# Raw weight slots and split halves: nine and six instead of eleven and four, in a two-layer encoder with a mixture of experts

## The chip, the core and the metric

The kernel runs on one core of a Trainium2 chip. The metric is the device time of one execution in microseconds (us); lower is better. Engines are named as in the profile: PE multiplies matrices, DVE, ACT and POOL work elementwise, SP here only issues the transfers (DMAs) that bring weights from HBM into SBUF.

## The reference

A token sequence `x` (256 tokens, width 1024) and 256 memory tokens go through two layers: a convolution and pooling mixer, cross-attention and a dense SwiGLU in layer 0; a Conformer convolution module, cross-attention and a SwiGLU over eight experts with the top two per token in layer 1. Everything is float32. Cut to what matters here:

```python
def swiglu(xn, w_gu, w_down):
    g, u = jnp.split(xn @ w_gu, 2, axis=-1)
    return (jax.nn.silu(g) * u) @ w_down

def moe_swiglu(xn, router, w_gu, w_down):
    logits = (xn @ router).astype(jnp.float32)
    top_v, top_i = lax.top_k(logits, TOP_K)
    w = jax.nn.softmax(top_v, axis=-1)
    comb = jnp.sum(jax.nn.one_hot(top_i, N_EXPERTS) * w[..., None], axis=-2)
    for e in range(N_EXPERTS):
        out = out + comb[..., e:e + 1] * swiglu(xn, w_gu[e], w_down[e])
    return out

h = h + even_mixer(...)              # layer 0
h = h + cross_attn(...); h = h + swiglu(...)
h = h + conformer_conv(...)          # layer 1
h = h + cross_attn(...); h = h + moe_swiglu(...)
return rmsnorm(h, final_norm)
```

## The kernel before

**Chunks.** All large weights come in chunks of 128 partitions by 2048 float32 (1 MB) through `load` (L143), which takes a slot of the pool `rawp` (tag "raw", `NRAW` = 11 slots, L86) or, for some chunks of the experts, a "spare" tile of the pool `big`, and issues the DMA on SP.

**Splitting.** PE multiplies in a rounded format, so that each weight w is used as a high part hi (w rounded) and a remainder lo (w minus hi). `split` (L152) makes both for the two halves of a chunk: ACT casts hi (L168), DVE subtracts for lo (L169). A half of hi is a tile of `hip`, a half of lo one of `lop`, both with `NPART` = 4 slots (L87, L88), so two chunks stand split at a time. A raw slot is free again when the DVE has made the last lo from it; a pair of halves is free when PE has used it.

**Other users of raw slots.** In the last product of layer 0 (`ffn_down`, L685 to L706) three chunks of `wv` are loaded and split beside it into `raw_pair` tiles (L198, class `Early`, L179): six raw slots, held until the values of layer 1 are multiplied (L803 to L828). The split of the last chunk of `wk` (L734) puts its second half into one more raw slot (`apart`, L161). The eight `pw1` chunks of the Conformer module are multiplied whole (`product_whole`, L250), out of their raw slots, which come free only when PE is done with them.

**The experts.** `expert` (L1112) runs eight times, with 42 chunks each: seven steps j, each with four chunks for gate and up (`gate_up`, L1117) and, one step behind, two for down (`down`, L1165). Such a group of six chunks is called a round below. Five experts are wide (positions 0, 1, 3, 5, 7 in this order): three matmuls per weight tile, 12 of 512 columns a chunk (`moving`, L207). Three are narrow (2, 4, 6): two matmuls, 8 a chunk (`narrow`, L1103), and the fourth chunk of a step is not split but multiplied whole (L1124). After the gate, ACT and DVE make the activation: L1141, L1142, L1143, L1144 and L1148 in a narrow expert, L1146 and L1148 in a wide one. L1148 needs the finished up product.

**What sets the order.** Most engines' queues are put in order when the program is made, by the framework's scheduler, which runs a plan of the kernel on its own clock and gives out slots in it; each engine then runs its queue in that order on the chip. From L857 on SP's order is written out by hand: the program's order of the loads. `RING` (L55) says which expert chunk takes a raw slot (r) and which a spare (s); from then on each chunk repeats the kind of the one `NRAW` + 6 = 17 before (L927), and so waits for that one's slot. `NAHEAD` (L58) is how many of these loads stand ahead of the attention's output product (L929).

Of the kernel before, what the change touches and what calls it, by code (L numbers as in the profile page):

```python
# [49 lines left out]
HALF = CAP // 2  # L50
TCKW = dict(schedule_with_timeline_sim=True)
NCKW = dict(dynamic_dma_scratch_size=512)
NRAW = 11
NPART = 4
RING = "rrrrrrrrsssssrrrrrs"  # L55
P2_POOL = (0, 2, 4, 6)
NWARM = 10
NAHEAD = 13  # L58
G_TAPS = 4 * (11, 12)


# [20 lines left out]
def _build(ctx, tc, io, cap):  # L82
    nc = tc.nc
    PSUM = bass.MemoryType.PSUM
    const = ctx.enter_context(tc.tile_pool(name="const", bufs=1))
    rawp = ctx.enter_context(tc.tile_pool(name="rawp", bufs=NRAW))  # L86
    hip = ctx.enter_context(tc.tile_pool(name="hip", bufs=NPART))  # L87
    lop = ctx.enter_context(tc.tile_pool(name="lop", bufs=NPART))  # L88
    big = ctx.enter_context(tc.tile_pool(name="big", bufs=10))
# [53 lines left out]
    def load(ap, n=CH, pieces=1, spare=False):  # L143
        raw = big_tile("spare") if spare else rawp.tile([P, CH], F32, tag="raw", name="raw")
        for i in range(pieces):
            sl = slice(i * n // pieces, (i + 1) * n // pieces)
            nc.sync.dma_start(raw[:, sl], ap[:, sl])
        return raw
# [772 lines left out]
    ahead = deque()  # L921
    kinds = list(RING)

    def fetch():
        n, (ap, pieces) = next(source)
        ahead.append(load(ap, pieces=pieces, spare=kinds[n] == "s"))
        kinds.append(kinds[-(NRAW + 6)])  # L927

    for _ in range(NAHEAD):  # L929
        fetch()  # L930
# [559 lines left out]
```

## Time and profile before

| what | value |
|---|---|
| time, median of 3 runs | 1550.54 us (1549.85 to 1551.14) |
| the profiled execution | 1551.01 us |
| its span | 1549.3 us |
| mean granted clock of PE | 0.994 of full speed |
| instructions | 23644 |
| read from HBM | 448.75 MB |

The page of the profile gives busy times and shares. The trace behind it is read by views: the sums of an engine's work in given stretches, the waits of one engine, the DMA issues, the timeline (instructions in order of time, with like ones merged as "x3", and in brackets the idle time before one and what ended it), and the chain of waits (the work that ended last, followed back from the end). Layer 0 takes about the first 390 us, the Conformer module and the attention run to about 594 us, the experts from there to about 1535 us. PEld is PE's loading of stationary tiles, SPq the SP queue.

### The profile page before, as it was taken

To read this page: it belongs to the slowest core of one execution; us is meant where nothing else is said; L and a number is where in the kernel's file an instruction comes from. 1 tells how busy PE (TensorE), PEld (TensorE's weight loads), DVE (VectorE), ACT (ScalarE), POOL (GpSimd) and SP (SyncE) were. 2 spreads that over 40 slices of the span, in tenths; PEclk is the share of its full clock that TensorE was granted. 3 is DMA by queue.
4 is the path that set the end of the run, shared out by engine and by line. 5 is a ranking of instruction groups with operands and counts; after the bars stand their busy time and mean duration, and the time that the engine had idled before them with its cause. 6 is when DMAs were issued, how large, how long until landed. Compare 5 with 4: busy or idle time off the path is not lost.

```text
span 1549.3 us, 23644 instructions
## 1 busy us (share of the span) xinstructions
PE 1513.3 (98%) x8558; PEld 1295.2 (84%) x8558; DVE 1298.1 (84%) x1730; ACT 1052.1 (68%) x1381; POOL 149.0 (10%) x230
## 2 busy tenths in 40 slices
PE   8899999999999999999999999999999999999996
PEld 8899999999998998888888778888667888667885
DVE  7866677776898868989989989889889888889897
ACT  6454554455575657777777877777777777777775
POOL 4710000001294210000000000000000000000000
PEclk9999999999999999999999999999999999999998
DMA  9654454436545566999999999999999999999940
GB/s 371 266 181 159 146 176 166 138 98 226 210 137 222 186 254 217 378 370 335 373 374 336 402 422 407 382 364 341 406 395 378 370 362 341 403 398 371 387 177 30
DMA packets 65214, 451.43 MB, mean 291 GB/s; under 512 B 7360, under 2 KB 7488, under 8 KB 12480
## 3 DMA queue, kind: packets, MB, share of 16 engines
q1 hardware_dynamic: 65088, 449.83, 76.7%
q8 instruction: 69, 1.13, 0.3%
q14 instruction: 57, 0.47, 0.1%
HBM read 448.75 MB, written 1.05 MB: 290 GB/s over the span
## 4 chain that ended last, share of the span: by engine, by line
PE 81%; DVE 9%; POOL 3%; issue 3%; ACT 2%; DMA 1%; SPq 0%; DVEq 0%; POOLq 0%; ACTq 0%
PE gu L211 8%; PE gu L212 8%; PE gu L216 8%; PE acc L205 7%; PE acc L204 7%; PE acc L203 7%; DVE lo L169 7%; PE gu L1124 5%; PE gu L1108 4%; PE py L211 4%; PE py L216 4%; PE py L212 4%; PE py L1108 3%; POOL part L764 2%; PE gx L1027 1%
## 5 line engine op out<-in xcount | busy, mean ns | idle before, releaser
L169 DVE TENSOR_TENSOR lo<-raw,hi 128x1024 fp32r<-128x1024 f32 (+3 forms) x573 | 671.0, 1208 | 120.1 <-ACT hi L168 110.4
L168 ACT CAST hi<-raw 128x1024 fp32r<-128x1024 f32 (+3 forms) x573 | 565.6, 1031 | 213.5 <-PE acc L204 92.0
L169 DVE TENSOR_TENSOR lo<-spare,hi 128x1024 fp32r<-128x1024 f32 (+1 forms) x226 | 261.4, 1203 | 24.6 <-ACT hi L168 20.5
L168 ACT CAST hi<-spare 128x1024 fp32r<-128x1024 f32 (+1 forms) x226 | 221.5, 1036 | 23.6 <-PE gu L212 11.9
L211 PE MATMUL gu<-hi,xg 128*128 128x512 f32 x560 | 218.8, 391 | 0.0
L212 PE MATMUL gu<-hi,xg 128*128 128x512 f32 x560 | 218.4, 390 | 0.0
L216 PE MATMUL gu<-lo,xg 128*128 128x512 f32 x560 | 154.2, 391 | 0.7 <-DVE lo L169 0.7
L216 PEld LDWEIGHTS gu<-lo,xg 128*128 128x128 f32 x560 | 104.7, 188 | 23.9 <-DVE lo L169 1.9
L211 PEld LDWEIGHTS gu<-hi,xg 128*128 128x128 f32 x560 | 105.1, 188 | 22.2 <-ACT hi L168 0.2
L212 PEld LDWEIGHTS gu<-hi,xg 128*128 128x128 f32 x560 | 105.1, 188 | 21.8
L211 PE MATMUL py<-hi,ht 128*128 128x512 f32 x280 | 111.1, 398 | 0.0
L212 PE MATMUL py<-hi,ht 128*128 128x512 f32 x280 | 109.3, 390 | 0.0
L205 PE MATMUL acc<-a2h,lo 128*128 128x256 f32 x336 | 95.2, 283 | 0.0
L204 PE MATMUL acc<-a2l,hi 128*128 128x256 f32 x336 | 95.2, 283 | 0.0
L203 PE MATMUL acc<-a2h,hi 128*128 128x256 f32 x336 | 95.1, 283 | 0.0
L1386 POOL TENSOR_TENSOR fo<-accum,fn 128x512 f32<-128x512 f32 x2 | 2.5, 1268 | 949.1 <-DVE accum L1190 949.1
L1108 PE MATMUL gu<-lo,xg 128*128 128x512 f32 x252 | 80.3, 411 | 8.0 <-DVE lo L169 8.0
L216 PE MATMUL py<-lo,ht 128*128 128x512 f32 x280 | 84.0, 395 | 0.0
L1108 PE MATMUL gu<-hi,xg 128*128 128x512 f32 x252 | 71.2, 396 | 0.0
L1108 PEld LDWEIGHTS gu<-lo,xg 128*128 128x128 f32 x252 | 43.4, 188 | 31.6 <-DVE lo L169 25.2
L203 PEld LDWEIGHTS acc<-a2h,hi 128*128 128x128 f32 x336 | 64.5, 192 | 0.0
L205 PEld LDWEIGHTS acc<-a2h,lo 128*128 128x128 f32 x336 | 64.5, 192 | 0.0
(421 smaller groups left out, 3176.9 us busy)
## 6 DMA issues: line engine op xcount, KB each, us to landing
raw<-in_moe_gu SPq DMA_DIRECT2D x139, 1024.0 KB, 7.1
spare<-in_moe_gu SPq DMA_DIRECT2D x85, 1024.0 KB, 7.2
raw<-in_moe_down SPq DMA_DIRECT2D x78, 1024.0 KB, 7.3
spare<-in_moe_down SPq DMA_DIRECT2D x32, 1024.0 KB, 7.0
raw<-in_ffn_gu SPq DMA_DIRECT2D x22, 1024.0 KB, 4.8
raw<-in_pw SPq DMA_DIRECT2D x12, 1024.0 KB, 4.9
raw<-in_ffn_down SPq DMA_DIRECT2D x16, 704.0 KB, 4.1
raw<-in_wk SPq DMA_DIRECT2D x8, 1024.0 KB, 7.1
```

Source lines behind the costliest of these rows:

```text
L168: done[:] = (S.copy(hi[:, i:i + step], raw[:, a + i:a + i + step]), V.tensor_sub(lo[:, i:i + step], raw[:, a + i:a + i + step], f32(hi[:, ...
L169: V.tensor_sub(lo[:, i:i + step], raw[:, a + i:a + i + step], f32(hi[:, i:i + step])))
L203: PE.matmul(ps, a[0], b[0], start=first, stop=False)
L204: PE.matmul(ps, a[0], b[1], start=False, stop=False)
L205: PE.matmul(ps, a[1], b[0], start=False, stop=last)
L211: PE.matmul(ps, a[0], b[0], start=first and i == 0, stop=False)
L212: PE.matmul(ps, a[1], b[0], start=False, stop=False)
L216: ins = PE.matmul(ps, a[0], b[1], start=False, stop=last and i == n - 1)
L764: G.tensor_add(part, part, prod)
L1027: PE.matmul(px[:, kk * P:(kk + 1) * P], xt[:, t * D + d0:t * D + d0 + P], oh[:, t, :], start=t == 0, stop=t == 1)
L1108: ins = PE.matmul(ps, x, w[part], start=first and i == part == 0, stop=last and part == 1 and i == n - 1)
L1124: PE.matmul(pz, f32(xs[kk]), w[:, kk * 512:(kk + 1) * 512], start=False, stop=kk == 3)
```

## The change

Two raw slots of 8 KB per partition are given up, and two halves each of hi and lo, of 4 KB per partition each, are added. Three chunks can then stand split instead of two. The pattern of kinds is shortened to a period of 15 (9 raw slots and 6 spares), and one load less stands ahead of the output product.

```diff
-NRAW = 11
-NPART = 4
-RING = "rrrrrrrrsssssrrrrrs"
+NRAW = 9
+NPART = 6
+RING = "rrrrrrrsssssrrrrs"
...
-NAHEAD = 13
+NAHEAD = 12
```

## Rows read from the trace of the kernel before

**Rows 1.** The page's part 1: busy us, share of the span, instructions.

```profile
PE 1513.3 (98%) x8558; PEld 1295.2 (84%) x8558; DVE 1298.1 (84%) x1730; ACT 1052.1 (68%) x1381; POOL 149.0 (10%) x230
```

**Rows 2.** Stretches: us, busy PE, PEld, DVE, ACT, POOL, clock, DMA, GB/s.

```profile
100.00:400.00 300.00, 300.00 (x2417) 296.03 (x2416) 206.76 (x322) 156.55 (x241) 14.67 (x16) 1.00 0.48 163
...
717.00:832.00 115.00, 115.00 (x526) 95.20 (x525) 105.44 (x101) 89.69 (x96) 0.00 (x0) 1.00 0.96 359
...
1065.00:1175.00 110.00, 105.85 (x438) 72.76 (x437) 94.32 (x98) 83.07 (x101) 0.00 (x0) 1.00 0.97 383
1185.00:1297.00 112.00, 111.80 (x525) 92.81 (x524) 100.95 (x97) 83.97 (x93) 0.00 (x0) 1.00 0.97 365
```

**Rows 3.** SP's own waits: us in total, times, longest.

```profile
SPq L147 <- DVE lo L169: 839.0, 307, 14.6
```

**Rows 4.** DMA issues: count, KB each, median us to landing.

```profile
raw<-in_moe_gu SPq DMA_DIRECT2D x139, 1024.0 KB, 7.1
...
raw<-in_pw SPq DMA_DIRECT2D x12, 1024.0 KB, 4.9
```

**Rows 5.** Timeline of SP in expert 2: two loads.

```profile
847.42 0.33 SPq L147 DMA_DIRECT2D spare<-in_moe_gu  x1
...
876.43 0.33 SPq L147 DMA_DIRECT2D spare<-in_moe_gu  x1
```

**Rows 6.** Timeline in expert 2: PE and ACT take these chunks.

```profile
886.25 3.59 PE L1124 MATMUL gu<-spare,xg 128*128 128x512 f32 x8
...
907.90 2.01 ACT L168 CAST hi<-spare 128x1024 fp32r<-128x1024 f32 x2
```

**Rows 7.** Chain of waits in expert 2: whole chunks, steps 3-6.

```profile
886.41 3.43 PE gu L1124 x8
...
899.41 3.43 PE gu L1124 x8
...
913.08 3.45 PE gu L1124 x8
...
928.64 3.43 PE gu L1124 x8
```

**Rows 8.** Chain of waits in expert 4: whole chunks, steps 1, 6.

```profile
1085.45 3.45 PE gu L1124 x8
...
1163.60 3.43 PE gu L1124 x8
```

**Rows 9.** Timeline of DVE in expert 4, step 3.

```profile
1118.11 1.22 DVE L169 TENSOR_TENSOR lo<-spare,hi 128x1024 fp32r<-128x1024 f32 x1 [1.72 <-ACT hi L168]
1120.06 0.75 DVE L1148 SCALAR_TENSOR_TENSOR eh<-gu,cw,esg 128x512 f32<-128x512 f32 x1 [0.73 <-PE gu L1124]
```

**Rows 10.** Timeline of ACT in expert 4, around L1141 of step 4.

```profile
1122.55 5.79 ACT L168 CAST hi<-raw 128x1024 fp32r<-128x1024 f32 x6
...
1129.91 0.59 ACT L1141 COPY esg<-gu 64x512 f32<-64x512 f32 x1 [1.57 <-PE gu L1108]
...
1132.62 1.98 ACT L168 CAST hi<-raw 128x1024 fp32r<-128x1024 f32 x2
```

**Rows 11.** Timeline of ACT in expert 2, around L1141 of step 4.

```profile
895.80 2.00 ACT L168 CAST hi<-spare 128x1024 fp32r<-128x1024 f32 x2 [0.88 <-PE gu L1108]
898.09 0.58 ACT L1141 COPY esg<-gu 64x512 f32<-64x512 f32 x1 [0.29 <-PE gu L1108]
```

**Rows 12.** Timeline of ACT in the wide experts 1 and 3.

```profile
756.78 2.96 ACT L168 CAST hi<-raw 128x1024 fp32r<-128x1024 f32 x3 [0.58 <-PE gu L212]
...
1013.52 0.69 ACT L1146 ACTIVATE esg<-gu,cw 128x512 f32<-128x512 f32 x1 [2.37 <-PE gu L216]
```

**Rows 13.** Timeline of PE and of SP in the Conformer module.

```profile
399.23 34.70 PE L255 MATMUL acc<-a,raw 128*128 128x256 f32 x160
...
434.20 7.07 PE L255 MATMUL acc<-a,raw 128*128 128x256 f32 x32
...
405.75 50.56 SPq L147 DMA_DIRECT2D raw<-in_pw  x10
```

## The prediction

> **What bounds the kernel now.** I read the page first: PE is busy in nearly the whole span, but DVE is not far behind [rows 1], so the shares alone do not say who waits for whom. The sums by stretch separate the regimes [rows 2]. In layer 0 (100 to 400 us) PE is busy for all of its 300 us and the transfers use half of the DMA engines' time. In the wide expert 1 PE is again busy for the whole stretch; in the narrow expert 4 it is not (105.85 of 110 us), and neither DVE (94.32) nor ACT (83.07) is full. The DMA share of 0.96 or 0.97 there tempts one to call the experts bound by transfers. Three views say no. SP's waits are for DVE's lo, that is, for a slot to come free: 839 us in 307 waits [rows 3]. So it is the slots that hold the loads back. A load lands 7.1 us after its issue in the median [rows 4]; the one issued at 847.42 us [rows 5] is multiplied whole at 886.25 [rows 6], 39 us later, and the one issued at 876.43 [rows 5] is cast at 907.90 [rows 6], 31.5 us later. The second is about the tightest chunk in the experts, and it still lies ready for some 24 us.
>
> What does bound a narrow expert is read from its rounds. On the chain of waits the whole chunks of expert 2 follow each other by 13.0 and 13.7 us, and then by 15.56 [rows 7]; in expert 4 five rounds from 1085.45 to 1163.60 take 78.15, or 15.63 each [rows 8]. Expert 6 is like expert 4. A late round thus costs 15.6 - 13.3 = 2.3 us more than an early one (13.3 is the mean of the first two). The timeline shows where: DVE stands still for 1.72 us until ACT has cast the next hi, and for 0.73 us behind L1148, which needs the up product [rows 9]; together 2.45. ACT is late because L1141, which waits 1.57 us for PE, stands ahead of those casts in its queue [rows 10]. In the early rounds of expert 2 the casts stand ahead of L1141 [rows 11].
>
> **The change part by part.** The sum is made on the profiled execution, 1551.01 us (span 1549.3 and 1.7 around it); the median of the runs is 0.47 lower.
>
> *Two raw slots fewer, in the experts.* A chunk could be loaded 17 + 2 = 19 ahead of PE (slots and split chunks), and afterwards 15 + 3 = 18. One chunk less is 2.2 to 2.6 us less of lead (a round of 13.3 or 15.6 over six chunks); two chunks less, where the third split chunk is not in use, are at most 5.2. The tightest chunk keeps over 18 us. What hides this is the ready ring, and the cost is 0. Were that cover gone, a chunk would cost what is left of its 7.1 us landing [rows 4].
>
> *A third split chunk, in wide experts and layer 0.* ACT does wait for PE to free halves there (0.58 us in expert 1 [rows 12]), so ACT and DVE will run further ahead. But PE, the one that ends the stretch, has no gap to give back: 115.00 of 115 us, and 300.00 of 300 [rows 2]. In the wide expert 3 ACT runs with less lead (it waits 2.37 us for PE at L1146 [rows 12]), and expert 5, in the same order, still has PE busy in 111.80 of 112 us [rows 2]. So lead is worth at most the 0.2 us left, in each wide expert. Cost 0, bounds -1 and 0.
>
> *A third split chunk, in late narrow rounds.* This decides the sign. The casts behind L1141 do not wait for a pair of halves: once ACT gets to them at 1132.62 no wait stands before them [rows 10], and their chunks landed long ago. They stand late because the queue was written so. The six casts at 1122.55 [rows 10] are the four of the gate's chunks and two more, so the plan is two halves ahead at L1141; so it is in every late round that I counted. In expert 2 the pair at 895.80 [rows 11] comes on top: four ahead, under the same four slots. A limit that did not change cannot have made the difference; I take it that in the plan the chunks themselves run out from step 5 of expert 2 on. More halves do not bring a planned chunk sooner, so I take 0 for experts 3 to 7. Bounds: 0, and eleven late rounds (one in expert 2, five each in 4 and 6) at 2.3, which is -25.
>
> *When the plan runs out.* If the 19 chunks of lead are used up over the 42 + 42 + 31 chunks to that point, one chunk less moves it forward by 115 / 19 = 6 chunks, one round of expert 2, at 2.3 us. Consumption there is faster than in the wide experts before it, so that six is the upper end of this estimate: I take two thirds, **+1.5**. Bounds: 0, and all five early rounds of expert 2 turned late, +11.5.
>
> *Raw slots in the Conformer module.* Of 9 slots six are held by the `wv` pairs and one by `apart`; two are left for the `pw1` chunks where there were four. PE takes 34.70 / 5 = 6.94 us for one of them [rows 13], and a load lands 4.9 us after its issue [rows 4]. With two slots the next chunk is loaded while PE uses the other, with 2.0 us to spare: 0. The cover is one slot thick. Bounds: 0, and two products, while `wk` and `wv` loads hold the other slot, that each wait 4.9, +9.8. In layer 0's last product, beside the `wv` pieces, two to four slots are left for chunks of 704 KB that are split well ahead of PE: 0, or one landing of 4.9 at most. The ten `pw` loads of SP's queue [rows 13] move as a block, and the loads behind them are wanted only after the Conformer module: 0. One load fewer ahead of the output product, and the shorter pattern, move loads within a queue that only waits for slots: 0.
>
> Sum: 1551.01 + 1.5 = 1552.5 by the profile, 1552.0 against the median.
>
> **The rivals.**
>
> *The halves bring the casts forward (faster).* With six halves the plan puts the casts ahead of L1141 and late rounds fall to the early 13.3. For it: the gaps of 1.72 and 0.73 repeat in each late round [rows 9], and ACT has idle time to fill [rows 10]. Against it: what is said of the lead above. Full price 25: 1525.5. Half of it, in one expert, gives 1538. The Trainium skill (Perfetto Trace Analysis, Optimization Strategy) says that the same gap repeated over a stretch can mean that SBUF has no room for the next tile; by it the gap would go and the time would be this rival's. The rows that speak against it are those of the casts without a wait.
>
> *Expert 2 turns late as a whole (slower).* The plan runs out at step 0 or 1 of expert 2, as the two slots lost count fully and the third split chunk is not filled. Five rounds at 2.3: 1562; two rounds give 1555. For it: the ring is what carries the lead from the wide experts into expert 2, and the plan there is near its end. Against it: six chunks of shift for each chunk of lead is already the upper end, so five rounds need the loss of five. It decides from a loss of two, which turns two rounds.
>
> *`pw1` runs on one slot (slower).* 1562 by two waits of 4.9, decided at the third product, about 413 us.
>
> That the change does not do what it says is inside my forecast: a third pair of halves exists, and PE never feels it.
>
> **How the numbers follow.** About 0.2% (3.1 us) is what a measurement of this kernel can tell from no change. My forecast, 1552.0 with its own range 1548 to 1555, has a chance of 0.52, of which 0.04 falls on either side of the band. The casts forward have 0.20, all faster. Expert 2 late has 0.15 (0.13 slower, 0.02 within), `pw1` on one slot 0.13 (0.11 slower, 0.02 within). That makes faster 0.24, same 0.48, slower 0.28. The range takes in both slower cases and the half gain in one expert, and leaves out the full gain: 1538 to 1562.
>
> **What would show it.** Right: in experts 4 and 6 the whole chunks still follow each other by 15.6 us, with L1141 ahead of the casts and ACT idle before it; the first late round of expert 2 comes one step earlier; chunks are cast at least 18 us after landing; `pw1` products follow each other by 6.9 us. Wrong: rounds near 13.3 in expert 4 (the order did hang on the halves), rounds of 15.6 from the start of expert 2, a PE gap of 2 us or more between two `pw1` products, or a load in the experts that PE, ACT or DVE waits for.

## The result and the profile after

The changed kernel is slower. Its median is 1562.54 us against 1550.45 us for the kernel before, a ratio of 1.0077 (95% interval 1.0059 to 1.0094). The forecast was 1552.0 (1538 to 1562) with "no change" as the likeliest case: the direction was missed, and the time lies half a microsecond above the range.

The page hides the loss. This is part 1 of the page of the kernel after, with the columns of [rows 1]:

```profile
PE 1519.2 (97%) x8558; PEld 1295.5 (83%) x8558; DVE 1298.7 (83%) x1730; ACT 1048.1 (67%) x1381; POOL 151.1 (10%) x230
```

The span is 1560.8 us, 11.5 longer. PE is busy 5.9 us longer with the same instructions, which means that it worked more slowly somewhere; the other 5.6 us it stood. The stretches of the kernel after, each put at the same place in its work as in [rows 2], say where it is not:

```profile
100.00:400.00 300.00, 300.00 (x2411) 295.81 (x2410) 206.78 (x324) 152.62 (x233) 16.48 (x16) 1.00 0.47 159
720.00:835.00 115.00, 115.00 (x522) 95.00 (x521) 105.42 (x102) 89.40 (x97) 0.00 (x0) 1.00 0.94 353
1076.00:1186.00 110.00, 105.94 (x434) 72.63 (x434) 94.82 (x99) 83.16 (x101) 0.00 (x0) 1.00 0.97 386
1196.00:1308.00 112.00, 111.79 (x522) 92.65 (x521) 102.01 (x99) 82.74 (x93) 0.00 (x0) 1.00 0.97 363
```

Layer 0, the wide expert 1, the narrow expert 4 and the wide expert 5 are as they were. So I laid the start times of the same instruction in both traces beside each other. A difference that stays the same from one row to the next means that nothing is lost between them:

| instruction | before, us | after, us | after - before |
|---|---|---|---|
| last matmul of `w_out` | 104.57 | 102.84 | -1.73 |
| second `pw1` product | 406.14 | 404.41 | -1.73 |
| third `pw1` product | 413.05 | 416.49 | +3.44 |
| fourth `pw1` product | 419.95 | 426.37 | +6.42 |
| eighth `pw1` product | 448.88 | 455.29 | +6.41 |
| last query product of layer 1 | 546.56 | 551.52 | +4.96 |
| first gather of expert 0 | 590.60 | 597.83 | +7.23 |
| L1148 of expert 1, step 6 | 828.34 | 834.86 | +6.52 |
| L1148 of expert 2, step 3 | 890.13 | 897.22 | +7.09 |
| L1148 of expert 2, step 6 | 932.11 | 943.65 | +11.54 |
| L1148 of expert 7, step 6 | 1522.54 | 1534.12 | +11.58 |

Four places change the difference by more than a microsecond to the bad: two `pw1` products, the last part of the attention of layer 1, and expert 2. Two change it to the good: the first 100 us, and the stretch between the eighth `pw1` product and the query products, by 1.45 us.

**The `pw1` products.** The timeline of SP (start, length from first to last issue, count) in the kernel after:

```profile
377.67 5.73 SPq L147 DMA_DIRECT2D raw<-in_pw  x2
385.54 0.33 SPq L147 DMA_DIRECT2D raw<-in_wk  x1
400.83 0.33 SPq L147 DMA_DIRECT2D raw<-in_wv  x1
404.60 0.33 SPq L147 DMA_DIRECT2D raw<-in_wk  x1
411.51 2.41 SPq L147 DMA_DIRECT2D raw<-in_pw  x2
```

Six of the nine slots hold the `wv` pairs and two the first `pw1` chunks, so one slot is left for the two `wk` loads and the `wv` load that stand ahead of the third `pw1` load in SP's queue. The first `wk` chunk takes it. The `wv` load at 400.83 waits until that chunk has been split, and DVE does this only behind the `a3` operations of L726 (timeline of DVE, same kernel):

```profile
395.64 2.85 DVE L726 SCALAR_TENSOR_TENSOR a<-hT,vec,rb 128x256 f32<-128x256 f32 x7
398.42 2.35 DVE L169 TENSOR_TENSOR lo<-raw,hi 128x1024 fp32r<-128x1024 f32 x2
```

The last `wk` load goes at 404.60 into the slot of the first `pw1` chunk, which PE has just left, and the slot of the `wv` chunk goes to the `apart` half. The third `pw1` chunk is left with the slot of the second and is issued at 411.51, when PE is done with that. In the kernel before it was issued at 405.75 [rows 13].

The timeline of PE at that place, and the stretches around it with the columns of [rows 2]:

```profile
416.49 11.78 PE L255 MATMUL acc<-a,raw 128*128 128x256 f32 x40 [5.01 <-ACT prod L763]
```

```profile
411.00:416.00 5.00, 0.48 (x3) 0.07 (x1) 5.00 (x10) 4.31 (x11) 3.30 (x4) 0.95 0.73 244
416.00:421.00 5.00, 4.51 (x11) 3.65 (x12) 5.00 (x14) 1.39 (x3) 4.53 (x7) 0.50 0.44 179
421.00:424.00 3.00, 3.00 (x13) 2.52 (x11) 3.00 (x9) 0.00 (x0) 0.38 (x1) 0.77 0.00 0
424.00:427.00 3.00, 3.00 (x15) 2.66 (x14) 1.71 (x5) 0.37 (x1) 0.00 (x0) 1.00 0.00 0
```

PE stands for 5.01 us. The row puts that down to ACT's L763, one of several things that the matmul waits for; but the load was issued 4.98 us before the matmul and landed 4.84 us after its issue, 0.14 us before it. Then comes a loss that no wait shows: the third product takes 9.88 us (416.49 to 426.37) instead of 6.91, since the granted clock is 0.50 up to 421 us and 0.77 in the next three. That is 3.0 us, about half of the longer busy time of part 1. The fourth product had its data in time.

**Expert 2.** ACT's timeline at L1141 of steps 3 and 4, to be held beside [rows 11]:

```profile
891.33 0.58 ACT L1141 COPY esg<-gu 64x512 f32<-64x512 f32 x1 [2.45 <-PE gu L1108]
...
893.89 3.88 ACT L168 CAST hi<-raw 128x1024 fp32r<-128x1024 f32 x4
...
906.52 0.58 ACT L1141 COPY esg<-gu 64x512 f32<-64x512 f32 x1 [0.77 <-PE gu L1108]
```

L1141 waits for PE, and the casts come behind it. Counted in halves whose casts stand ahead of it, beyond those that the gate itself needs, the lead at L1141 through the seven steps of expert 2 was 5 4 5 5 4 2 2 and is 6 6 4 2 2 2 2. The lead of 2, and with it the late rounds, begins two steps earlier. In experts 4 and 6 the lead is 2 throughout, as before.

**The attention of layer 1.** DVE's timeline while PE waits for `pT`, and PE's:

```profile
561.85 4.62 DVE L169 TENSOR_TENSOR lo<-raw,hi 128x1024 fp32r<-128x1024 f32 x4
566.39 0.68 DVE L269 TENSOR_TENSOR pT<-pT 128x512 fp32r<-128x512 f32 x1
```

```profile
567.13 0.39 PE L204 MATMUL po<-pT,vh 128*128 128x256 f32 x1 [1.64 <-DVE pT L269]
```

Four `lo` of the `wo` chunks stand ahead of the `lo` of `pT`. In the kernel before two stood there (556.90 to 559.25 us), and so it is in the run with four halves and nine slots (below).

### The profile page after: what moved, and what is told of

Its sections match the earlier page's. It is cut to its first block, busy times and chain, and to the rows that moved or that the text cites. A ratio compares the mean times of both kernels' runs of the same rounds, so it can differ in the third digit from the quotient of the medians.

```text
span 1560.8 us, 23483 instructions
## 1 busy us (share of the span) xinstructions
PE 1519.2 (97%) x8558; PEld 1295.5 (83%) x8558; DVE 1298.7 (83%) x1730; ACT 1048.1 (67%) x1381; POOL 151.1 (10%) x230
## 4 chain that ended last, share of the span: by engine, by line
PE 78%; DVE 12%; issue 4%; POOL 3%; ACT 2%; DMA 1%; SPq 0%; DVEq 0%; POOLq 0%; ACTq 0%
PE gu L216 8%; PE gu L211 8%; PE gu L212 8%; DVE lo L169 8%; PE acc L204 7%; PE acc L203 7%; PE acc L205 7%; PE gu L1124 4%; PE py L211 4%; PE py L216 4%; PE py L212 4%; PE gu L1108 3%; PE py L1108 2%; DVE cacc L770 2%; PE acc L255 2%
## 5 line engine op out<-in xcount | busy, mean ns | idle before, releaser
L169 DVE TENSOR_TENSOR lo<-raw,hi 128x1024 fp32r<-128x1024 f32 (+3 forms) x557 | 645.4, 1196 | 100.0 <-ACT hi L168 93.0
L168 ACT CAST hi<-raw 128x1024 fp32r<-128x1024 f32 (+3 forms) x557 | 543.1, 1024 | 190.1 <-PE acc L204 77.2
L169 DVE TENSOR_TENSOR lo<-spare,hi 128x1024 fp32r<-128x1024 f32 x242 | 283.4, 1218 | 33.9 <-ACT hi L168 31.7
L168 ACT CAST hi<-spare 128x1024 fp32r<-128x1024 f32 x242 | 238.6, 1049 | 24.8 <-PE gu L212 15.9
L216 PE MATMUL py<-lo,ht 128*128 128x512 f32 x280 | 79.8, 391 | 0.0
L764 POOL TENSOR_TENSOR part<-part,prod 128x256 f32<-128x256 f32 x84 | 61.3, 745 | 48.1 <-ACT prod L763 44.0
```

The costliest lines, as they stand in the source:

```text
L168: done[:] = (S.copy(hi[:, i:i + step], raw[:, a + i:a + i + step]), V.tensor_sub(lo[:, i:i + step], raw[:, a + i:a + i + step], f32(hi[:, ...
L169: V.tensor_sub(lo[:, i:i + step], raw[:, a + i:a + i + step], f32(hi[:, i:i + step])))
L216: ins = PE.matmul(ps, a[0], b[1], start=False, stop=last and i == n - 1)
L764: G.tensor_add(part, part, prod)
```

## Experiments

**Slots or halves: nine slots with four halves.**

```diff
 NRAW = 9
-NPART = 6
+NPART = 4
```

(against the kernel after; the shortened order stays)

> Nine raw slots with the shortened order, but four halves each as before. Theory (the loss comes from the raw slots: some 8 us of PE waits at the third and fourth pw1 product, and expert 2's casts falling behind two rounds earlier, some 5 us; the halves are worth nothing beyond the 1.7 us by which layer 0 ended earlier): 1562 to 1565 us, pw1 products 2 and 3 each behind a PE gap of 3 to 5 us, narrow rounds of expert 2 at 15 us or more from step 3 or 4 on. Rival (it is the halves that make the schedule worse, by letting ACT and DVE run far ahead): 1549 to 1553 us.

Measured: 1560.95 us, ratio to before 1.0061 (1.0047 to 1.0075). Against the kernel before, the start times differ by -0.06 us at the second `pw1` product, +4.94 at the third, +8.00 at the fourth, +7.23 at the first gather, +7.26 at the end of expert 1 and +10.18 at the end of expert 2. The time is a microsecond below the range expected and far from the rival's. So the slots, with their order, cost 10.3 of the 11.5 us in the span by themselves, and the halves are not the main cause. What six halves add to this is worked out from the two runs: 1.7 us gained in the first 100 us, some 2.3 lost in the attention, 0.7 gained in experts 0 and 1, and 2.1 more lost in expert 2 (5.0 against 2.9), though the lead there falls to 2 at the same step in both; why these rounds cost more is not shown. In the attention this run has two `lo` ahead of `pT` and no PE wait of a microsecond. Timeline of DVE, this run:

```profile
564.13 2.35 DVE L169 TENSOR_TENSOR lo<-raw,hi 128x1024 fp32r<-128x1024 f32 x2
566.40 0.69 DVE L269 TENSOR_TENSOR pT<-pT 128x512 fp32r<-128x512 f32 x1
```

The expectation spoke of two PE gaps; the second is the clock here too (0.50 in the five microseconds after the wait).

**A slot given back to `pw1`, from the halves.**

```diff
-        k1.append(split(load(io["wk"][1, 3]), apart=(1,)))
+        k1.append(split(load(io["wk"][1, 3])))
```

(against the kernel after)

> The changed kernel, with the second half of the last wk chunk split into a fifth pair of halves instead of into a raw slot, so that pw1 has three raw slots and not two. Theory (slot shortage in the Conformer module): the PE gap before the fourth pw1 product (3.0 us) goes, and of that before the third (5.2 us) most; expert 2 stays as late as in the changed kernel: 1554 to 1558 us. Rival (the waits at pw1 come from the wk splits standing late behind the a3 operations, which a slot more does not mend): 1561 to 1564 us.

Measured: 1561.40 us, 1.0068 (1.0054 to 1.0082). Between the second and the fourth `pw1` product the kernel loses 4.68 us instead of 8.15: one wait, and 1.8 us of lower clock after it. The timeline of PE names the transfer this time:

```profile
413.75 10.56 PE L255 MATMUL acc<-a,raw 128*128 128x256 f32 x40 [2.76 <-DMA raw<-in_pw]
```

SP shows why the slot helped by so little: the `wv` load is still issued only at 400.35, because `apart` took its slot only after those three loads, so that leaving it out frees nothing for them. The total did not follow, as the attention then lost 4.0 us instead of 2.3 (the same four `lo`, and a lower clock after the wait). My 1554 to 1558 was wrong on both counts. The time is the rival's, 1561 to 1564, and half of its reason holds: the `wk` split behind L726 is what keeps the `wv` load back until 400.35. The other half does not: a slot more does mend it where those loads can use it (the run with ten slots, below).

**The loads moved out of the way.**

```diff
-    pw1 = [load(io["pw1"][c]) for c in range(2)]
+    pw1 = [load(io["pw1"][c]) for c in range(3)]
...
-        ps = product_whole(pw1[c] if c < 2 else load(io["pw1"][c]), whole_of(a3))
+        ps = product_whole(pw1[c] if c < 3 else load(io["pw1"][c]), whole_of(a3))
+        if c == 7:
+            rest_of_kv()
```

(against the kernel after; `rest_of_kv` holds the three loads with their splits, unchanged)

> The changed kernel with the last two wk chunks and the last wv chunk loaded and split behind the eighth pw1 product instead of ahead of the third, so that pw1 has three raw slots to itself. Theory (the PE waits at pw1 come from those loads holding its slots): both gaps (5.2 and 3.0 us) go, pw1 products follow each other by 6.9 us; what comes of it depends on whether DVE, nearly full with the convolution until 475 us, takes the moved splits without delay: 1554 us if it does, up to 1562 if their ten us of DVE end up behind the convolution. Rival (the gaps come from a3 being late or from the transfers): the gaps stay, 1562 us or more.

Measured: 1564.84 us, 1.0091 (1.0078 to 1.0105), 2.8 us above the slowest time that the theory allowed. Timeline of PE:

```profile
397.10 34.70 PE L255 MATMUL acc<-a,raw 128*128 128x256 f32 x160
...
465.42 1.22 PE L777 MATMUL mu<-cv,ones 128*128 128x256 f32 x2 [5.43 <-DVE cv L774]
...
486.34 0.70 PE L777 MATMUL mu<-cv,ones 128*128 128x256 f32 x2 [1.96 <-DVE cv L774]
```

The first five products take 34.70 us, as in [rows 13]: with three slots to themselves they never wait. So the gap came from those three loads and not from a late `a3`, nor from the transfers being slow. The splits now stand in DVE's queue beside the convolution, and PE waits for that instead, 5.43 and 1.96 us. The place where the loads stood was the right one; they needed slots there.

**One slot less instead of two.**

```diff
-NRAW = 11
+NRAW = 10
-RING = "rrrrrrrrsssssrrrrrs"
+RING = "rrrrrrrrsssssrrrrs"
-NAHEAD = 13
+NAHEAD = 12
```

(against the kernel before)

> Ten raw slots, four halves, order of sixteen: half of what the run with nine slots takes away. Theory (slots alone): three slots for pw1, PE gaps at its third and fourth product of together 4 to 5 us as in the run with the freed slot (2.9 and 1.8) against 8.0 with nine; expert 2 later by about half of the 2.9 us: 1554.5 to 1557.5 us. Rival (a threshold: only the loss of the second slot costs): 1550 to 1552 us.

Measured: 1558.33 us, 1.0048 (1.0035 to 1.0062), 0.8 us above the expected range, and for other reasons. The timeline of SP in this run:

```profile
387.22 0.33 SPq L147 DMA_DIRECT2D raw<-in_wk  x1
391.18 0.33 SPq L147 DMA_DIRECT2D raw<-in_wv  x1
403.22 0.33 SPq L147 DMA_DIRECT2D raw<-in_wk  x1
406.27 7.30 SPq L147 DMA_DIRECT2D raw<-in_pw  x3
```

With one slot more the `wv` load passes at 391.18, the third `pw1` load goes at 406.27, and no product waits: the difference to the kernel before is -0.06 us from the second `pw1` product to the eighth. In the Conformer module the tenth slot is enough, as the rival had it there; its total, 1550 to 1552, failed. All 8 us are lost between step 5 of expert 1 and the end of expert 2: the lead falls to 4 and 2 at steps 5 and 6 of expert 1 and is 2 at every step of expert 2. Half the loss of slots, and nearly three times the loss in expert 2 of the run with nine: the number of slots alone cannot be what decides there.

**The order alone, shortened.**

```diff
-RING = "rrrrrrrrsssssrrrrrs"
+RING = "rrrrrrrsssssrrrrs"
-NAHEAD = 13
+NAHEAD = 12
...
-        kinds.append(kinds[-(NRAW + 6)])
+        kinds.append(kinds[-15])
```

(against the kernel before: eleven slots, of which the experts use nine)

> The kernel before with its eleven raw slots and four halves, and only the order of the experts' chunks shortened to 15 (nine raw, six spare), so that two raw slots go unused there. Theory (expert 2's order hangs on how many chunks the ring carries): pw1 as before, expert 2 gains two late rounds at 2.3 us: 1554 to 1557 us. Rival (expert 2 turned late because all of it starts 7 us later, or because of the halves): 1549 to 1552 us.

Measured: 1554.38 us, 1.0023 (1.0014 to 1.0032). `pw1` is as before. The difference to the kernel before goes from -0.65 us at the end of expert 1 to +2.25 at the end of expert 2, and the lead there is 5 4 5 2 2 2 2, as with nine slots and four halves. The run ends 3.3 us later than the kernel before; the 1.2 us that are lost behind the last expert have no cause here. So the two losses are separate: the slots cost in the Conformer module, the order in expert 2.

**The order alone, same length, five of the six spares one place later.**

```diff
-RING = "rrrrrrrrsssssrrrrrs"
+RING = "rrrrrrrrrsssssrrrrs"
```

(against the kernel before)

> The kernel before, eleven raw slots, four halves, the same period of seventeen with eleven raw and six spare, only the five spares begin one place later in it. Theory as it stands after the run with ten slots (not the number of slots, but how raw and spare slots alternate decides when the written lead runs out): the lead at L1141 is 4 at step 0 of expert 2 and 2 from step 1 on, so four to five more late rounds at 2.3 us: 1558 to 1562 us. Rival (the number of chunks that the slots hold decides): 1550 to 1551 us, expert 2 as before.

Measured: 1557.30 us, 1.0043 (1.0029 to 1.0056), with the same slots, halves and period; 0.7 us below the range, and far from the rival's. The lead is 4 at step 0 of expert 2 and 2 from step 1 on, as expected. Timeline of ACT in expert 2, steps 1 to 3:

```profile
855.68 0.58 ACT L1141 COPY esg<-gu 64x512 f32<-64x512 f32 x1 [2.24 <-PE gu L1108]
...
870.18 0.59 ACT L1141 COPY esg<-gu 64x512 f32<-64x512 f32 x1 [1.47 <-PE gu L1108]
...
885.74 0.58 ACT L1141 COPY esg<-gu 64x512 f32<-64x512 f32 x1 [1.57 <-PE gu L1108]
```

L1141 waits for PE from step 1 on, as it does in late rounds [rows 10], and expert 2 costs 6.9 us more. Nothing else was changed, so here the place of the spare slots in the period decides when the late order begins.

**Ten slots, spares in one block.**

```diff
-RING = "rrrrrrrrsssssrrrrs"
+RING = "rrrrrrssssssrrrrrr"
```

(against the run with ten slots)

> Ten raw slots and four halves as in the run that gave 1558.3, the six spares in one block that begins two places earlier. Theory (alternation): lead of 4 to 6 in all of expert 2, no late round there, pw1 without a wait as in that run: 1545 to 1548 us, faster than the kernel before with a slot less. Rival (number): 1556 us or more.

Measured: 1549.23 us, 0.9991 (0.9982 to 1.0000): the tenth slot's 8 us are back, and the kernel before is matched with a slot less. It is less than I expected. The lead stays at 4 to 6 in all of expert 2, but its steps 1 to 6 take 69.9 us against 69.5 before. Its rounds take 13.4 us to steps 3 and 4, and 14.0 and 15.0 us to steps 5 and 6. The 13.3 of the forecast was read from rounds in which the lead fell; a lead that falls by two halves spares DVE two `lo` of 1.2 us, once, so part of what made those rounds short was lead being spent. What this run gained came later, in expert 3 (from +0.35 us at the end of expert 2 to -1.65), where its lead came down to 2 at step 6.

**The changed kernel, spares in one block.**

```diff
-RING = "rrrrrrrsssssrrrrs"
+RING = "rrrrrrssssssrrrrr"
```

(against the kernel after)

> The changed kernel (nine raw slots, six halves), the six spares in one block that begins one place earlier. Theory (alternation for expert 2, slots for the Conformer module): pw1 keeps its 8.2 us of waits; expert 2 has its lead of 6 or 7 up to step 5, so the two late rounds that the change added go and one more: 1555 to 1558 us. Rival (number): 1562 us.

Measured: 1555.91 us, 1.0033 (1.0021 to 1.0045), as expected. The `pw1` loss is still there (+6.19 us at the fourth product); expert 2 now takes 0.9 us less than before instead of 5.0 more. So another order of the same slots takes back 6.6 of the 12.1 us that the change cost: the 5.0 of expert 2 and somewhat more. What stays is lost before the experts, by the number of slots in the Conformer module and by the halves in the attention. That the number has no share in the experts is not shown: with the spares in one block the lead comes down to 2 at step 6 of expert 2 with nine slots and six halves, and at step 6 of expert 3 with ten and four.

**The casts put ahead of L1141.** The late rounds themselves were open to the same kind of edit:

```diff
...
+                    nxt = chunk()
+                    ready.append(nxt)
                     for kk in range(4):
                         PE.matmul(pz, f32(xs[kk]), w[:, kk * 512:(kk + 1) * 512],
...
-                S.copy(sg[:HALF], pg[HALF:])
+                with tc.issue_after(done[0].ins):
+                    S.copy(sg[:HALF], pg[HALF:])
```

(against the kernel before; `chunk` takes from `ready` first, so the next chunk is split ahead of the gate)

> The kernel before, with the casts of the next chunk put ahead of L1141 in every narrow round, by an order between instructions alone. Theory (a late round costs 2.3 us more than an early one only because L1141 stands ahead of those casts): late rounds fall from 15.6 to 13.3 to 14.3 us, some eleven of them: 1525 to 1540 us. Rival (early rounds are short because they use up the lead that the wide experts built, and a standing round of 15.6 us is what DVE and PE need): 1546 to 1553 us.

Measured: 1544.13 us, 0.9956 (0.9942 to 0.9969): faster than the rival allowed, but short of the expected gain. Narrow rounds take 15.2 us, not 13.3 to 14.3. DVE no longer waits at L1148; it waits one instruction further on:

```profile
1123.26 0.43 DVE L1039 TENSOR_TENSOR ht<-ht 128x256 fp32r<-128x256 f32 x1 [1.42 <-ACT ht L1038]
1124.21 6.90 DVE L169 TENSOR_TENSOR lo<-raw,hi 128x1024 fp32r<-128x1024 f32 x6 [0.52 <-ACT hi L168]
```

ACT's L1038 waits for PE's transposed rows, and the casts of the second gate chunk stand behind it: the stall of [rows 9], moved.

**And ahead of L1038.**

```diff
-                return side_by_side(ht[:, o:o + 512], pt[:, :4 * HALF])
+                with tc.issue_after(done[0].ins):
+                    return side_by_side(ht[:, o:o + 512], pt[:, :4 * HALF])
```

(on top of the edit before)

> As the run with the casts put first (the kernel before, four halves, eleven raw slots), and L1038, the cast of the transposed rows, is put behind the casts of the second gate chunk as well. Theory (with the casts put first a narrow round took 15.2 us, since DVE then stood 1.4 and 0.5 us behind L1038; it is again an order in ACT's queue): rounds of 13.5 to 14.3 us, 1526 to 1535 us. Rival (a standing narrow round needs some 15 us, and the stall only moves to the next wait): 1541 to 1546 us.

Measured: 1530.40 us, 0.9872 (0.9857 to 0.9887), 20 us below the kernel before and 32 below the changed one. DVE at two successive L1155 (the line of L1148 in this kernel) in expert 4:

```profile
1099.86 0.75 DVE L1155 SCALAR_TENSOR_TENSOR eh<-gu,cw,esg 128x512 f32<-128x512 f32 x1
...
1112.91 0.74 DVE L1155 SCALAR_TENSOR_TENSOR eh<-gu,cw,esg 128x512 f32<-128x512 f32 x1
```

A standing round takes 13.05 us where it took 15.57, with the same slots, halves and instructions. From step 1 to step 6 expert 4 takes 68.6 us instead of 78.1. One of these rounds, from step 4 to step 5, still takes 16.14 us (15.89 before): DVE's L1083 stands ahead of the `lo` there and waits 2.52 us for PE. Late rounds were late by the order in the queues alone: ACT's was edited, and DVE's `lo`, which follow the casts, moved with it.

**Both orders with six halves and nine slots.**

```diff
-        k1.append(split(load(io["wk"][1, 3]), apart=(1,)))
+        k1.append(split(load(io["wk"][1, 3])))
```

(the kernel after with this and the two edits above)

> The changed kernel (nine raw slots, six halves, the last wk chunk's second half not in a raw slot) with both orders between instructions in the narrow rounds. Theory (the halves are worth something in the late rounds only where the order uses them): narrow rounds as in the run of the same orders with four halves or up to 0.5 us shorter, the rest as in the run without that raw slot held (1561.4): 1535 to 1546 us. Rival (six halves with the orders run PE dry of nothing more, and the time lost before the experts stays): the same gain as with four halves, less or more by under 2 us; so the two differ by 8 to 12 us.

Measured: 1540.56 us, 0.9936 (0.9922 to 0.9949). The difference to the run before it is 10.2 us, as the rival had it; the theory's range held this time too. Expert 4 takes 68.6 us from step 1 to step 6, as with four halves: a third split chunk is worth nothing there with this order either.

## Why the prediction was wrong

**What bounds the kernel** held. It said that a late narrow round is late because of the order in ACT's queue and not for want of data or of halves. Six halves left the rounds at 15.56 us, and moving two instructions made most of them 13 us. Here the Trainium skill's reading of a gap that repeats (Perfetto Trace Analysis, Optimization Strategy: perhaps no room in SBUF for the next tile) would have had six halves close it; the measurement decides against it in this case.

**Two raw slots fewer, in the experts: 0**, **the third split chunk in wide experts: 0**, **in late rounds: 0.** Right, by [rows 2] against the stretches after, by the lead of 2 that stayed in experts 4 and 6, and since no wait of PE, ACT or DVE in the experts goes back to a load.

**Raw slots in the Conformer module: 0 (bounds 0 and +9.8).** This is the step that failed. It let the `pw1` chunks alternate over two slots "with 2.0 us to spare", as if they stood alone in SP's queue. Three other loads stand ahead of the third chunk and take the slots first; I had them only in the upper bound. What it measured is +8.15 us, in one wait of 5.0 and 3.0 us of lower clock, not in two waits of 4.9. A PE gap of 2 us or more between two `pw1` products was named as a sign of being wrong. The rival `pw1` on one slot named the place and the product and was given 0.13. That its time, 1562, came out is luck: it had 9.8 us from `pw1` and nothing else but the 1.5, where the runs show 8.15 and five other terms that happen to add up to the rest.

**When the plan runs out: +1.5 (bounds 0 and +11.5).** The place was right, the size not: +5.0. The rule behind it, that the chunks which the slots hold are spent evenly over 115 chunks, fell. It gave one late round more; there were two. Nor is 2.3 us the price of each: two more late rounds cost 5.0 with six halves and 2.9 with four, and four more cost 6.9 in the run with the spares one place later. With ten slots the lead came down to 2 at step 6 of expert 1, 36 chunks earlier than with eleven; with nine only 12 chunks earlier; and with eleven slots and the spares one place later 24. How raw and spare slots alternate moves that place by itself. What in the plan answers to that is not settled: the traces show the order that the plan wrote and not what it counted on.

**A third split chunk where it does harm: not in the sum.** The `wo` splits planned ahead of `pT` cost 2.3 us. I looked for the halves' effect only where PE had no gap to lose, and asked of more lead what it would gain, not what it would stand in front of.

**Layer 0: bounds -1 and 0.** The two profiles differ by 1.7 before 105 us, ahead of the stretch from which the bounds were read: PE waits there 4.06 us for POOL's L593 and 0.95 for ACT's L168 with four halves, 2.32 for L593 and 1.84 for DVE's L263 with six. Kernels that are the same up to that place differed there by up to 1.4 us between profiles (0 to 1.4 earlier than the kernel before with four halves, 1.4 to 2.2 with six), so the size is rough.

The sum of the measured terms: -1.7 + 8.2 - 1.5 (won back between `pw1` and the query products, 0.97 of it a PE wait for DVE's L771 in the kernel before that is gone) + 2.3 - 0.7 (experts 0 and 1) + 5.0 = 11.6, against 11.5 in the span.

## What to carry to other kernels

Count the slots of a ring at the moment when the most loads want one, in the order of the queue that issues them, and give each load ahead of the critical one its slot first; a margin worked out for one stream alone is no margin. Where an order is written ahead of time, the pattern in which buffers of two kinds alternate can matter more than their number: hold the number fixed and vary the pattern before paying memory for it. And when every round shows the same gap, look at which instruction stands ahead of the late one in its queue and move that; here it was worth 20 us, and two more halves of each kind nothing.

## What was not expected of the hardware

Some waits of PE cost more than their length. After 5.01 us without work PE was granted 0.50 of its clock, the lower of its two levels, up to about 421 us, which made the product behind the wait 3.0 us longer; after 4.83 us in the run with nine slots and four halves the product lost 3.05, after 2.76 us in the run with the freed slot 1.8. Timeline stretches of that last run (columns of [rows 2]):

```profile
413.00:416.00 3.00, 2.25 (x6) 1.83 (x7) 3.00 (x8) 2.29 (x6) 2.74 (x4) 0.64 1.07 391
416.00:419.00 3.00, 3.00 (x13) 2.52 (x12) 3.00 (x9) 1.02 (x2) 2.71 (x4) 0.79 0.78 306
```

Not every wait does this, and its length alone does not tell which: in the attention of the changed kernel PE waited 1.64 us and the clock stayed at 1.00 (564 to 570 us), in the run with the freed slot the same wait of 1.64 us was followed by 0.50 (564 to 567 us).

What a lower clock costs is booked as busy time, so it shows in no list of waits; the clock's column shows it. The Trainium skill (TensorE: Matmul & The Clock Gate, Part 1) says that the array runs at half rate after the engine has been idle; the rows of the changed kernel agree, with 0.50 after the 5.01 us, and the 1.64 us there show no such fall.
